# Second norm's output stored without a gap column; gated tiles stored in 64-byte steps

## The chip, the cores and the metric

One core of one Trainium2 chip runs the kernel. The metric is the time of one execution on the device in microseconds (us), taken as the median of several runs.

## The reference

One layer of a hybrid backbone for 640 tokens: 128 context tokens and 512 latent tokens, 1024 channels. A modulated norm, two token mixers (retention and attention), gates, an output projection with a residual; then a second modulated norm and a gated feed-forward part with a convolution of width 3 along the tokens, separately for context and latents; a last norm. What the change touches, cut to its core:

```python
def token_mixer(h, ...):
    ...
    y = sigmoid(ga) * (ya @ w_att_o) + sigmoid(gr) * (yr @ w_ret_o)
    return y @ w_out, ...

def conv_ffn(h, w_up, conv_w, conv_b, w_down):       # D_FF = 2816
    u = h @ w_up                                     # 1024 -> 2 x 2816
    up = jnp.pad(u, ((0, 0), (1, 1), (0, 0)))        # a zero token at both ends
    uc = conv_w[0] * up[:, :L] + conv_w[1] * up[:, 1:L + 1] + conv_w[2] * up[:, 2:L + 2] + conv_b
    a, g = jnp.split(uc, 2, axis=-1)
    return (jax.nn.silu(g) * a) @ w_down

def layer(x, ...):        # once for the context, once for the latents
    x = x + g1 * token_mixer(h, ...)
    h = rmsnorm(x, norm2_g) * (1.0 + sc2) + sh2
    x = x + g2 * conv_ffn(h, ...)
```

## The kernel before, in words

The 640 tokens are five tiles of 128: tile 0 the context, tiles 1 to 4 the latents. Both groups go through the same products at once. Each fp32 operand is split into a high part (rounded to TensorE's fp32r, a cast on ScalarE, "hi") and a low part (the rest, a subtraction on VectorE or an accumulating DMA, "lo"), and a product is three matmuls: hi x hi, hi x lo and lo x hi (`mm3`, L156 to L158).

`h2` is a pair (hi, lo) of arrays with channels on the partitions and tokens in the free dimension. It is used twice. First `merge` (L1101 to L1105) writes y into it, one block of 128 channels at a time, as the ret products of two blocks are done; the output projection then reads it as the stationary operand (`yk`), in `a_group` (first half of the output columns) and `out_half` (second half). After that, `h2_norm` and `h2_trans` write the second norm's output into it, tile by tile. It is 644 columns wide: the context at 0 to 127, a zero gap column at 128, the latents at 129 to 640, and three zero columns behind. The gap stands for the zero token between context and latents, so that one convolution over all columns serves both groups. VectorE writes these zeros once.

The feed-forward part makes 22 blocks of 128 channels of a and 22 of g. Blocks 0 and 1 of both are computed by `up_cols` in column pieces of 256 and 388 columns, as the tiles become ready; blocks 2 and 3 of a by a plain product in halves of 322 columns (`HW`); all others two at a time by `unit_group` (19 groups), seven products (m = 1, 5, 6, 2, 3, 7, 4) of four channel blocks over 322 columns in place of eight, with sums of the halves of h2 and of the weights made beforehand (`sums`, on VectorE and ScalarE; `PLAN` for the weights). Products 1, 6, 7 and 4 of a unit add up in one PSUM bank (named mm7.mm.n), which ScalarE reads in between: L1564 after m = 1, L1568 after m = 6, L1572 after m = 7 (a copy into a small constant array, const.u1), L1577 after m = 4. VectorE adds or subtracts the other terms (L1570 for m = 2, L1573 for m = 7, L1583 for m = 3). The result u is a row of 645 columns with a zero column at either end, read by `conv` (L1346 on ScalarE, L1347 and L1348 on VectorE) in 641 columns and three shifts. `gate` makes tanh (L1358), two products (L1359, L1360) and the hi and lo parts of the gated tile (L1361 on ScalarE, L1362 on VectorE) into gt0 and gt1, each of which holds a pair of blocks in 2 x 644 columns. The down projection reads tiles of 128 tokens from these as its stationary operand, four blocks at a time (`down_groups`), ten banks of 12 matmuls for each set of four blocks; `last_group` does the last four blocks. `down_sum` adds to the residual x1 on VectorE (L1435 to L1452).

TensorE's order is written out by hand: `groups` lists loads, weight preparations and product items, `seq` strings the items with m = 4 held back by two items, and `pump` lets preparations run ahead while eight weight slots (`wh`) are free. Raw weights have two slots (`raw`, loaded by SP's queue, L133), and are cast at L144 (hi) and L149 (lo), or L146 and an accumulating DMA of GpSimd (L147) for the lo part; in a unit at L1540 and L1545. In the feed-forward part a scheduler sets the order of ScalarE's and VectorE's instructions from its own costs; each engine works through its list in that order.

## Time and profile before

| what | value |
|---|---|
| median of 3 runs | 1170.83 us (1170.36 to 1171.75) |
| the profiled execution's span | 1169.8 us; about 1.0 us less than the median, which lies around the span |
| granted TensorE clock | 9 tenths or more of full speed in all 40 slices |
| PE, DVE, ACT, POOL busy | 98%, 66%, 51%, 15% of the span |
| output projection | about 657 to 720 us |
| second norm, first pairs of up-projection | about 690 to 770 |
| first down banks | 770 to 784 |
| units and down banks | 784 to 1130 |
| last down banks, residual, last norm | 1130 to the end |

PE is TensorE's matmuls, PEld its weight loads, DVE VectorE, ACT ScalarE, POOL GpSimd, SP SyncE; a q behind the name is the engine's queue. A row of the timeline has the start in us from the span's beginning, the duration, engine, line, operation, output <- inputs, the shape, and in brackets the idle time just before it and what ended that. Matmuls overlap, so their cost is read from start to start and not from the duration. The chain of waits is followed back from the last instruction: each piece is a start, a length and the work on which the rest waited.

### The profile page before, as it was taken

What the parts mean: (1) busy time and instruction counts of PE and PEld (TensorE: products, weight loads), DVE (VectorE), ACT (ScalarE), POOL (GpSimd) and SP (SyncE); (2) the same over time, 40 slices, a digit from 0 to 9 for tenths busy, and PEclk for the clock granted to TensorE, in tenths of its full rate; (3) what the DMA queues carried; (4) which work ended last, traced back from release to release, by engine and by line L of the source; (5) the groups of instructions that cost most, each with busy time, mean ns of one, the idle gap of its engine ahead of it and who ended that gap; (6) DMA issues with size and microseconds to landing.
All of it is one profiled execution on the core that took longest, in us unless ns stands there. A gap on an engine that the chain in (4) does not pass through costs nothing.

```text
span 1169.8 us, 18399 instructions
## 1 busy us (share of the span) xinstructions
PE 1143.2 (98%) x7269; PEld 1030.1 (88%) x7269; DVE 772.8 (66%) x1433; ACT 591.5 (51%) x1087; POOL 180.8 (15%) x194
## 2 busy tenths in 40 slices
...
PEclk9999999999999999999999999999999999999999
...
GB/s 306 244 136 72 38 36 37 37 35 217 261 175 171 176 76 76 37 37 36 71 38 148 267 110 200 110 83 124 153 132 134 143 136 168 127 117 153 136 110 125
DMA packets 135848, 145.85 MB, mean 125 GB/s; under 512 B 26561, under 2 KB 101393, under 8 KB 135761
## 3 DMA queue, kind: packets, MB, share of 16 engines
...
q8 instruction: 57, 0.93, 0.3%
...
## 4 chain that ended last, share of the span: by engine, by line
PE 80%; DVE 8%; ACT 5%; issue 3%; DMA 2%; POOL 1%; ACTq 0%; DVEq 0%; POOLq 0%
DMA f1.s.11_5326<-spill.u2.2_2889 1%; DMA f1.s.13_5328<-spill.u2.2_2889 1%; DVE x1.u1.1_6460 L1440 1%; DMA weights.raw.414_10840<-in_w_down 0%; POOL f0.s.5_3528 L955 0%; DMA const.u2.2_72<-in_b_mod 0%; DVE x1.u1.1_6460 L1489 0%; DVE x1.u1.1_6460 L1452 0%; ACT acts.u1.1_91 L1104 0%; DVE gt.gt0.5_7309 L1388 0%; DVE weights.raw.395_10492 L1537 0%; DVE x1.u1.1_6460 L1447 0%; DVE acts.u2.2_92 L414 0%; PE mm1.mm.11_295 L158 0%; PE mm7.mm.42_9455 L1559 0%
## 5 line engine op out<-in xcount | busy, mean ns | idle before, releaser
L796 POOL DMA_DIRECT2D spill.u2.2_2889<-f1.s.1_1161 x1 | 0.6, 588 | 130.2 <-DVE mod.u4.4_2848 L587 130.2
L1573 DVE TENSOR_TENSOR t7.u4.4_6978<-t7.u4.4_6978,const.u1.1_70 128x322 f32<-128x322 f32 x10 | 5.0, 496 | 11.8 <-ACT const.u1.1_70 L1572 11.8
L1085 POOL DMA_DIRECT2D weights.wh.164_5980<-weights.raw.156_5913 x1 | 1.3, 1347 | 69.6 <-DVE f1.s.9_5324 L1125 69.6
L892 DVE SCALAR_TENSOR_TENSOR ret2.u1.1_4325<-ret2.u1.1_4325,const.u13.13_88 64x128 f32<-64x128 f32 x24 | 6.8, 339 | 6.6 <-ACT ret2.u1.1_4325 L885 6.5
L894 DVE SCALAR_TENSOR_TENSOR ret2.u1.1_4325<-ret2.u1.1_4325,const.u13.13_88 64x128 f32<-64x128 f32 x24 | 6.6, 386 | 4.8 <-ACT ret2.u1.1_4325 L887 4.8
L842 DVE TENSOR_TENSOR ret.u5.5_3531<-ret.u5.5_3531,ret.u1.1_3524 128x512 f32<-128x512 f32 x5 | 3.5, 692 | 9.4 <-POOL ret.r2k.8_3709 L840 3.3
L842 DVE TENSOR_TENSOR ret.u4.4_3530<-ret.u4.4_3530,ret.u1.1_3524 128x512 f32<-128x512 f32 x5 | 3.5, 692 | 9.0 <-POOL ret.r2k.11_3889 L840 4.7
L566 POOL TENSOR_TENSOR p1.u1.1_605<-p1.u3.3_609,p1q.u1.1_599 128x512 f32<-128x512 f32 x1 | 1.3, 1310 | 43.9 <-DMA p1.u4.4_611<-in_cache_k 43.9
L149 DVE TENSOR_TENSOR weights.wh.108_4359<-weights.raw.106_4356,weights.wh.107_4358 128x1024 fp32r<-128x1024 f32 x1 | 1.2, 1224 | 10.3 <-ACT weights.wh.107_4358 L144 10.3
L144 ACT CAST weights.wh.112_4514<-weights.raw.111_4512 128x1024 fp32r<-128x1024 f32 x1 | 1.1, 1050 | 13.2 <-PE mm3.mm.36_4223 L157 13.2
L411 ACT CAST acts.u1.1_91<-f0.s.2_105 128x640 fp32r<-128x640 f32 x4 | 2.9, 728 | 9.5 <-DVE f0.s.2_105 L409 9.5
L259 DVE COPY mod2.wr.9_4315<-aux3.aux.15_4282 128x128 f32<-128x128 f32 x1 | 0.3, 291 | 10.9 <-PE aux3.aux.15_4282 L256 10.9
L428 PE MATMUL aux1.aux.1_135<-const.u1.1_70,const.u2.2_72 80*128 80x80 f32 x1 | 0.4, 365 | 7.0 <-DMA const.u2.2_72<-in_b_mod 7.0
L955 POOL TENSOR_TENSOR f0.s.5_3528<-f0.s.5_3528,ret2.ny20.13_4911 128x512 f32<-128x512 f32 x5 | 6.0, 1236 | 8.0 <-DVE ret2.ny20.13_4911 L219 8.0
L535 ACT ACTIVATE f0.s.3_711<-f0.s.3_711,p1q.ny20.11_879 128x128 f32<-128x128 f32 x20 | 6.0, 388 | 2.5 <-DVE p1q.ny20.11_879 L217 2.5
L144 ACT CAST weights.wh.67_3362<-weights.raw.66_3360 128x1024 fp32r<-128x1024 f32 x1 | 1.0, 1045 | 11.5 <-PE mm3.mm.8_3141 L195 11.5
L144 ACT CAST weights.wh.77_3617<-weights.raw.76_3615 128x1024 fp32r<-128x1024 f32 x1 | 1.0, 1045 | 11.5 <-PE mm3.mm.16_3454 L195 11.5
L144 ACT CAST weights.wh.72_3542<-weights.raw.71_3540 128x1024 fp32r<-128x1024 f32 x1 | 1.0, 1045 | 11.4 <-PE mm3.mm.12_3298 L195 11.4
L1451 DVE TENSOR_TENSOR x1.u1.1_6460<-x1.u1.1_6460,gate.u1.1_6447 128x512 f32<-128x512 f32 x10 | 6.8, 686 | 0.0
L144 ACT CAST weights.wh.92_3979<-weights.raw.91_3977 128x1024 fp32r<-128x1024 f32 x1 | 1.0, 1047 | 11.2 <-PE mm3.mm.26_3760 L157 11.2
L861 POOL MEMSET ret2.u2.2_4326<- 128x512 f32 x1 | 0.5, 525 | 38.9 <-PE aux3.aux.15_4282 L256 38.9
L1484 POOL TENSOR_TENSOR x1.u1.1_6460<-x1.u1.1_6460,weights.raw.422_11041 128x512 f32<-128x512 f32 x3 | 4.9, 1649 | 10.2 <-ACT x1.tm.112_11054 L1457 7.4
...
## 6 DMA issues: line engine op xcount, KB each, us to landing
...
p0.u6.6_126<-in_w_mod SPq DMA_DIRECT2D x2, 1024.0 KB, 15.2
p0.u7.7_129<-in_w_mod SPq DMA_DIRECT2D x2, 1024.0 KB, 12.1
...
```

The lines of the kernel that those rows point to most:

```text
L144: nc.scalar.copy(hi, rv)
L411: nc.scalar.copy(hT[0][:, k, :], xk)
L535: nc.scalar.activation(x[:, j], x[:, j], AF.Copy, scale=rstd[:, j:j + 1])
L566: nc.gpsimd.tensor_mul(ct, r2[:, :, 0, :], gqk[:, i:i + 1, :].to_broadcast([P, 4, P]))
L842: V.tensor_mul(z, z, r1[:, t, 0:1, :].to_broadcast([P, 8, 64]))
L892: V.scalar_tensor_tensor(Ss[0:64, hh, st + 1, j], Ss[0:64, hh, st, j], cdsel[0:64, h:h + 1], Ss[0:64, hh, st + 1, j], op0=ALU.mult, op1=AL ...
L894: V.scalar_tensor_tensor(Ss[64:128, hh, 2 - st, j], Ss[64:128, hh, 3 - st, j], cdsel[64:128, h:h + 1], Ss[64:128, hh, 2 - st, j], op0=ALU. ...
L955: nc.gpsimd.tensor_mul(ov, ov, rso[:, 4 * t:4 * t + 4].unsqueeze(2).to_broadcast([P, 4, P]))
L1440: V.tensor_add(x1[:, t, gs], x1[:, t, gs], down_mul(ps, t, c0))
L1451: V.tensor_mul(x1[:, t, gs], x1[:, t, gs], gb[:, t == 0, gs])
L1484: eng.tensor_mul(x, x, fg[:, c0:c0 + 512])
L1573: V.tensor_sub(u[1][:, hi_u], u[1][:, hi_u], u3[i])
```

## The change

`HW` becomes 320, and h2 has 640 columns without a gap.

- `merge` casts and subtracts a block of 640 columns in one instruction each, in place of 128 and 512.
- The zeroing of the gap columns (a memset and four copies on VectorE) goes.
- The output projection's tiles start at t x 128 in place of one column on, and so do the second norm's.
- `up_cols` computes 256 and 384 columns; the plain product and the units 2 x 320. The gap exists only in u: `u_parts` cuts a piece of columns that spans column 128 in two, so the lower half (0 to 319) is written as 128 + 192 columns by two instructions: on ScalarE for m = 1 and m = 6, on VectorE for m = 2 and m = 3.
- Zero columns of u are written once at the start by GpSimd (12 memsets in place of 4); VectorE's memsets behind m = 3, 7 and 4 go.
- The gated tiles lie in rows of 656 columns (`GW`), shifted by 15 columns: the latents' tiles start at 16 + 128 t columns, and the second block of a pair 656 columns on, which in bytes are multiples of 64; the context's tile starts at column 15. Before, they were at 0 and 129 + 128 (t - 1), the second block 644 on.

```diff
@@ shapes
-HW = 322
+HW = 320
+GW = 656
...
@@ def a_group
-                ts = slice(t * P + gap * (t > 0), (t + 1) * P + gap * (t > 0))
+                ts = slice(t * P, (t + 1) * P)
...
@@ def merge(f)
             c = 2 * p + f
-            for s_, d_ in ((slice(0, P), slice(0, P)), (slice(P, TOK), slice(P + 1, TOK + 1))):
-                nc.scalar.copy(h2[0][:, c, d_], u[f][:, s_])
-                V.tensor_sub(h2[1][:, c, d_], u[f][:, s_], h2[0][:, c, d_].bitcast(F32))
+            nc.scalar.copy(h2[0][:, c, :], u[f])
+            V.tensor_sub(h2[1][:, c, :], u[f], h2[0][:, c, :].bitcast(F32))
...
@@ def gt_pair()
-        return [gtp([P, 2, 2 * HW], F32R, tag=f"gt{i}", bufs=2) for i in range(2)]
+        return [gtp([P, 2, GW], F32R, tag=f"gt{i}", bufs=2) for i in range(2)]
...
@@ def h2_trans(t)
-        c0 = t * P + int(t > 0)
+        c0 = t * P
...
@@ ahead of out_half
-    zero = x_tmp()[:, :KD * 4].rearrange("p (k c) -> p k c", k=KD)
-    V.memset(zero, 0)
-    for h in h2:
-        V.tensor_copy(h[:, :, P:P + 1], zero[:, :, :1])
-        V.tensor_copy(h[:, :, TOK + 1:], zero[:, :, 1:])
@@ def out_half(t, h)
-            ts = slice(t * P + (t > 0), (t + 1) * P + (t > 0))
+            ts = slice(t * P, (t + 1) * P)
...
-            nc.gpsimd.memset(u[:, 0:1], 0)
+            for c in (0, P + 1, TOK + 2):
+                nc.gpsimd.memset(u[:, c:c + 1], 0)
+
+    def u_parts(u, lo, hi):
+        cuts = [lo] + [P] * (lo < P < hi) + [hi]
+        return [(u[:, x + 1 + (x >= P):y + 1 + (x >= P)], slice(x - lo, y - lo)) for x, y in zip(cuts, cuts[1:])]
...
@@ def up_cols
-        nc.scalar.copy(ub[f % 2][i][:, lo + 1:hi + 1], ps)
+        for d, sl in u_parts(ub[f % 2][i], lo, hi):
+            nc.scalar.copy(d, ps[:, sl])
...
@@ def gate(f)
-        r = [x[:, f % 2, :641] for x in gts[f // 2]]
+        r = [x[:, f % 2, 15:656] for x in gts[f // 2]]
...
@@ def down_mm
-        c0 = 0 if t == 0 else 129 + (t - 1) * P
+        c0 = 15 if t == 0 else 16 + t * P
...
@@ unit_group: def prod(m)
-        lo_u, hi_u = slice(1, 1 + HW), slice(1 + HW, 1 + 2 * HW)
+        los = [u_parts(x, 0, HW) for x in u]
+        his = [u_parts(x, HW, TOK)[0][0] for x in u]
...
                 if m == 1:
-                    nc.scalar.copy(u[0][:, lo_u], ps)
+                    for d, sl in los[0]:
+                        nc.scalar.copy(d, ps[:, sl])
...
                 elif m == 6:
-                    nc.scalar.activation(u[1][:, lo_u], ps, AF.Copy, scale=-1.0)
+                    for d, sl in los[1]:
+                        nc.scalar.activation(d, ps[:, sl], AF.Copy, scale=-1.0)
                 elif m == 2:
-                    V.tensor_add(u[0][:, lo_u], u[0][:, lo_u], ps)
+                    for d, sl in los[0]:
+                        V.tensor_add(d, d, ps[:, sl])
                 elif m == 7:
                     nc.scalar.copy(u3[i], ps)
-                    V.tensor_sub(u[1][:, hi_u], u[1][:, hi_u], u3[i])
-                    V.memset(u[1][:, 642:643], 0)
+                    V.tensor_sub(his[1], his[1], u3[i])
...
                 elif m == 4:
-                    nc.scalar.copy(u[0][:, hi_u], ps)
-                    V.memset(u[0][:, 642:643], 0)
+                    nc.scalar.copy(his[0], ps)
...
                 else:
-                    V.tensor_sub(u[1][:, lo_u], u[1][:, lo_u], ps)
-                    V.memset(u[1][:, 129:130], 0)
+                    for d, sl in los[1]:
+                        V.tensor_sub(d, d, ps[:, sl])
```

Behind the change lines move by one to five: L1346 is L1348, L1361 and L1362 are L1363 and L1364, L1572 and L1573 are L1578 and L1579, L144 is L145.

TensorE's and SP's orders are the same but for the sizes. ScalarE's and VectorE's lists change in length (ScalarE 939 to 971 rows, VectorE 1339 to 1307) and at a few places in order. Three of them follow.

ScalarE, where the first gate copies (L276) follow the sums of the halves, about 753 us (sums.u5 is the high part of a sum of halves of h2, x1.row the convolution's result). Before:

```order
L144 CAST weights.wh.219_7364<-weights.raw.215_7355 128x1024
L1339 COPY t7.u4.4_6978<-mm3.mm.92_7234 128x388
L1401 CAST sums.u5.5_6970<-gt.gt0.5_7309 128x1288
L1346 ACTIVATE x1.row.60_7273<-t7.u4.4_6978,t7.u5.5_6983 128x641
L276 COPY gate.u1.1_6447<-mm7.mm.1_7285 128x512
L276 COPY gate.u1.1_6447<-mm7.mm.2_7291 128x512
```

After:

```order
L145 CAST weights.wh.219_7354<-weights.raw.215_7345 128x1024
L1341 COPY t7.u4.4_6956<-mm3.mm.92_7224 128x384
L147 ACTIVATE weights.wh.220_7355<-weights.raw.215_7345 128x1024
L1348 ACTIVATE x1.row.59_7263<-t7.u4.4_6956,t7.u5.5_6969 128x641
L277 COPY gate.u1.1_6431<-mm7.mm.1_7275 128x512
L277 COPY gate.u1.1_6431<-mm7.mm.2_7281 128x512
L1403 CAST sums.u5.5_6948<-gt.gt0.5_7299 128x1280
```

The cast of the sum has moved behind two gate copies, and a weight's low part stands in its place.

ScalarE in the units, about 819 us, between the copy of an m = 7 product and the next m = 1 copies (u is t7.u1 to u4). Before:

```order
L1572 COPY const.u1.1_70<-mm7.mm.15_7859 128x322
L1346 ACTIVATE x1.row.67_7987<-t7.u4.4_6978,t7.u5.5_6983 128x641
L1564 COPY t7.u1.1_6975<-mm7.mm.18_7991 128x322
L144 CAST weights.wh.252_8033<-weights.raw.247_7895 128x1024
L146 ACTIVATE weights.wh.253_8034<-weights.raw.247_7895 128x1024
```

After:

```order
L1578 COPY const.u1.1_70<-mm7.mm.15_7854 128x320
L145 CAST weights.wh.252_8029<-weights.raw.247_7891 128x1024
L1348 ACTIVATE x1.row.66_7983<-t7.u4.4_6956,t7.u5.5_6969 128x641
L1568 COPY t7.u1.1_6953<-mm7.mm.18_7987 128x128
L1568 COPY t7.u1.1_6953<-mm7.mm.18_7987 128x192
L147 ACTIVATE weights.wh.253_8030<-weights.raw.247_7891 128x1024
```

The weight's cast has moved ahead of the convolution, and the m = 1 copy is two.

ScalarE behind the last unit's m = 6 product, where the last raw weights (raw.414) are cast. Before:

```order
L1568 ACTIVATE t7.u4.4_6978<-mm7.mm.63_10822 128x322
L1572 COPY const.u1.1_70<-mm7.mm.63_10822 128x322
L144 CAST weights.wh.416_10891<-weights.raw.414_10840 128x1024
L1346 ACTIVATE x1.row.109_10938<-t7.u4.4_6978,t7.u5.5_6983 128x641
L144 CAST weights.wh.418_11031<-weights.raw.407_10724 128x1024
L146 ACTIVATE weights.wh.419_11032<-weights.raw.407_10724 128x1024
L144 CAST weights.wh.420_11036<-weights.raw.414_10840 128x1024
L1577 COPY t7.u2.2_6976<-mm7.mm.63_10822 128x322
L1358 ACTIVATE t7.tg.26_10983<-x1.row.109_10938 128x641
L1346 ACTIVATE x1.row.110_10970<-t7.u2.2_6976,t7.u5.5_6983 128x641
L146 ACTIVATE weights.wh.421_11037<-weights.raw.414_10840 128x1024
```

After:

```order
L1573 ACTIVATE t7.u4.4_6956<-mm7.mm.63_10833 128x192
L145 CAST weights.wh.416_10903<-weights.raw.414_10852 128x1024
L1578 COPY const.u1.1_70<-mm7.mm.63_10833 128x320
L145 CAST weights.wh.418_11042<-weights.raw.407_10734 128x1024
L147 ACTIVATE weights.wh.419_11043<-weights.raw.407_10734 128x1024
L1348 ACTIVATE x1.row.108_10950<-t7.u4.4_6956,t7.u5.5_6969 128x641
L145 CAST weights.wh.420_11047<-weights.raw.414_10852 128x1024
L1582 COPY t7.u2.2_6954<-mm7.mm.63_10833 128x320
L147 ACTIVATE weights.wh.421_11048<-weights.raw.414_10852 128x1024
L1348 ACTIVATE x1.row.109_10981<-t7.u2.2_6954,t7.u5.5_6969 128x641
L1360 ACTIVATE t7.tg.26_10994<-x1.row.108_10950 128x641
```

The m = 7 copy has moved behind the cast of wh.416, and the convolution and tanh behind further casts. On VectorE the subtraction that reads that copy has moved behind the low part of the same weights. Before:

```order
L1573 TENSOR_TENSOR t7.u4.4_6978<-t7.u4.4_6978,const.u1.1_70 128x322
L1574 MEMSET t7.u4.4_6978 128x1
L149 TENSOR_TENSOR weights.wh.417_10892<-weights.raw.414_10840,weights.wh.416_10891 128x1024
L1347 SCALAR_TENSOR_TENSOR x1.row.109_10938<-t7.u4.4_6978,t7.u5.5_6983,x1.row.109_10938 128x641
L1348 SCALAR_TENSOR_TENSOR x1.row.109_10938<-t7.u4.4_6978,t7.u5.5_6983,x1.row.109_10938 128x641
```

After:

```order
L150 TENSOR_TENSOR weights.wh.417_10904<-weights.raw.414_10852,weights.wh.416_10903 128x1024
L1579 TENSOR_TENSOR t7.u4.4_6956<-t7.u4.4_6956,const.u1.1_70 128x320
L1349 SCALAR_TENSOR_TENSOR x1.row.108_10950<-t7.u4.4_6956,t7.u5.5_6969,x1.row.108_10950 128x641
L1350 SCALAR_TENSOR_TENSOR x1.row.108_10950<-t7.u4.4_6956,t7.u5.5_6969,x1.row.108_10950 128x641
L1349 SCALAR_TENSOR_TENSOR x1.row.109_10981<-t7.u2.2_6954,t7.u5.5_6969,x1.row.109_10981 128x641
```

Here wh.417 now comes ahead of the subtraction and the convolution behind both; x1.row.108 and 109 after are 109 and 110 before.

10 lines of the change are left out of this document (5 added, 5 removed).

## The prediction, made before the changed kernel was run

> **What bounds the kernel now.** The page comes first: the share of TensorE (PE), its clock, and who makes up the chain that ended last.
>
> ```profile
> PE 1143.2 (98%) x7269; PEld 1030.1 (88%) x7269; DVE 772.8 (66%) x1433; ACT 591.5 (51%) x1087; POOL 180.8 (15%) x194
> PEclk9999999999999999999999999999999999999999
> PE 80%; DVE 8%; ACT 5%; issue 3%; DMA 2%; POOL 1%; ACTq 0%; DVEq 0%; POOLq 0%
> ```
>
> Next the windows by stage (from:to, length, then busy time of PE, PEld, DVE, ACT, POOL, clock, DMA share, GB/s).
>
> ```profile
> 784.00:884.00 100.00, 99.87 (x606) 93.93 (x606) 77.49 (x135) 65.58 (x113) 18.11 (x16) 1.00 0.60 132
> 984.00:1084.00 100.00, 100.00 (x575) 91.72 (x574) 78.78 (x136) 57.23 (x97) 16.36 (x14) 1.00 0.64 143
> 1134.00:1170.00 36.00, 26.18 (x125) 21.24 (x124) 28.72 (x53) 16.21 (x35) 8.64 (x8) 0.92 0.40 117
> ```
>
> From 784 to 1084 PE is full at a granted clock of 1.00, while ACT and DVE have 20 to 40 us in 100 to spare: there a matmul saved is time saved. The end is different, as the chain of waits shows:
>
> ```profile
> 1091.21 0.16 PE mm7.mm.57_10456 L1562
> 1091.40 0.44 ACT const.u1.1_70 L1572
> ...
> 1125.55 0.61 DVE x1.row.108_10874 L1347
> 1126.15 5.13 DMA weights.raw.414_10840<-in_w_down
> 1131.28 0.02 issue
> 1131.31 1.05 ACT weights.wh.416_10891 L144
> ...
> 1143.61 0.84 DVE gt.gt1.28_10982 L1362
> ```
>
> The chain leaves PE at 1091.40 and runs by ACT, DVE and one weight load to the last gated tile, 1144.45. So PE time saved before 1091 counts: DVE and ACT then start their last stretch sooner, and the load, which waits for DVE at 1126.15, goes out sooner with them. PE time saved after 1091 doesn't count, and ACT and DVE work between the load's landing (1131.31) and 1144.45 counts in full. The waits of PE's weight loads, 600 to the end (line, releaser: total, times, longest us), name the larger stalls that are left, three before 1091 and one (acc.51) in the end itself:
>
> ```profile
> PEld acc7.acc.11_8140 L158 <- DVE gt.gt1.12_8069 L1362: 0.6, 1, 0.6
> PEld acc7.acc.51_10942 L158 <- DVE gt.gt1.28_10982 L1362: 0.6, 1, 0.6
> PEld mm7.mm.5_7371 L1336 <- ACT gate.u1.1_6447 L276: 0.4, 1, 0.4
> PEld aux3.aux.90_6532 L274 <- ACT gate.u1.1_6447 L276: 0.4, 1, 0.4
> ```
>
> **Columns.** What the change removes first is two columns of every matmul over h2. PE's timeline (start, duration) has the 322-column products of the feed-forward part and the 320-column products of an earlier stage, both in gapless runs:
>
> ```profile
> 561.75 0.31 PE L194 MATMUL mm3.mm.49_5476<-acts.u1.1_91,weights.wh.134_5338 128*128 128x320 f32 x1
> 608.83 0.31 PE L1114 MATMUL mm3.mm.63_5899<-yr.u1.1_5318,weights.wh.152_5832 128*128 128x320 f32 x1
> ...
> 783.69 0.31 PE L1559 MATMUL mm7.mm.9_7597<-acts.u1.1_91,weights.wh.222_7483 128*128 128x322 f32 x1
> 831.51 0.40 PE L156 MATMUL acc7.acc.11_8140<-weights.wh.252_8033,gt.gt0.9_7787 128*128 128x512 f32 x1
> ```
>
> 321 matmuls start in the first 47.08 us, 146.67 ns each; 324 in the second 47.82, 147.59 each. The difference is 0.92 ns a matmul, 11.0 ns a product of 12, and the ratio is 322/320 to four digits. Of 19 x 7 = 133 products 126 lie before 1091.40: **1.39 us**. The plain up group's 96 matmuls add **0.09**. (The Trainium skill, "TensorE: Matmul & The Clock Gate", Back-to-back issue gap, has a warm gap of N/2.4 + 2.5 ns, so 0.83 ns for two columns; the sum would be 1.26 in place of 1.39. The rows are nearer to pure proportion.)
>
> **Alignment.** Runs of 512-column matmuls, from a start to the first row behind the run:
>
> ```profile
> 525.95 0.39 PE L156 MATMUL mm3.mm.44_5150<-weights.wh.122_5155,acts.u1.1_91 128*128 128x512 f32 x1
> 548.14 0.30 PE L194 MATMUL mm3.mm.47_5346<-acts.u1.1_91,weights.wh.132_5334 128*128 128x320 f32 x1
> ...
> 676.81 0.40 PE L156 MATMUL mm3.mm.75_6473<-weights.wh.190_6448,acts.u1.1_91 128*128 128x512 f32 x1
> 690.75 0.40 PE L156 MATMUL mm3.mm.80_6679<-weights.wh.194_6647,acts.u1.1_91 128*128 128x512 f32 x1
> ...
> 769.83 0.39 PE L156 MATMUL acc7.acc.1_7502<-weights.wh.216_7357,gt.gt0.7_7325 128*128 128x512 f32 x1
> ...
> 839.40 0.39 PE L156 MATMUL acc7.acc.13_8190<-weights.wh.252_8033,gt.gt0.9_7787 128*128 128x512 f32 x1
> 847.78 0.31 PE L1559 MATMUL mm7.mm.21_8240<-acts.u1.1_91,weights.wh.259_8090 128*128 128x322 f32 x1
> ```
>
> With tiles at multiples of 128 columns (525.95) 96 matmuls take 22.19 us, 2774 ns per 12. The output projection, whose tiles stand one column on (676.81), has 60 in 13.94: 2788. The down banks (839.40) have 36 in 8.38: 2793. But the first down banks, 769.83 to 783.69, read tiles just as shifted and take 60 in 13.86: 2772. So alignment is one candidate for these 14 to 19 ns and not a proven one. If it is the cause, the 240 matmuls of the output projection give back 0.28 and the 35 four-f down banks before 1091 give 0.67; if not, nothing. I take **0.2** of 0 to 0.28, since the whole run there is slow, and **0.35** of 0 to 0.67, half, because of the contrary run. The Trainium skill, "SBUF — State Buffer", Operand start alignment, says of element alignment that "This is about legality, not speed"; it knows no such price, and by it both terms would be nothing.
>
> **Merges, splits and gates** on ACT:
>
> ```profile
> 665.54 0.82 ACT L1104 CAST acts.u1.1_91<-f1.s.13_5328 128x128 fp32r<-128x128 f32 x2 [4.71 <-DMA f1.s.13_5328<-spill.u2.2_2889]
> 667.71 1.04 ACT L144 CAST weights.wh.190_6448<-weights.raw.188_6438 128x1024 fp32r<-128x1024 f32 x1
> ...
> 750.48 1.05 ACT L146 ACTIVATE weights.wh.217_7358<-weights.raw.210_7343 128x1024 fp32r<-128x1024 f32 x1
> 752.79 1.27 ACT L1401 CAST sums.u5.5_6970<-gt.gt0.5_7309 128x1288 fp32r<-128x1288 f32 x1
> ...
> 819.30 0.43 ACT L1572 COPY const.u1.1_70<-mm7.mm.15_7859 128x322 f32<-128x322 f32 x1 [0.67 <-PE mm7.mm.15_7859 L1562]
> 820.30 0.93 ACT L1346 ACTIVATE x1.row.67_7987<-t7.u4.4_6978,t7.u5.5_6983 128x641 f32<-128x641 f32 x1 [0.56 <-DVE t7.u4.4_6978 L1573]
> L411 ACT CAST acts.u1.1_91<-f0.s.2_105 128x640 fp32r<-128x640 f32 x4 | 2.9, 728 | 9.5 <-DVE f0.s.2_105 L409 9.5
> L861 POOL MEMSET ret2.u2.2_4326<- 128x512 f32 x1 | 0.5, 525 | 38.9 <-PE aux3.aux.15_4282 L256 38.9
> ```
>
> The change makes one cast of each pair of merge casts. Three split merges take 665.54 to 667.71, 0.72 each. One 640-wide cast is 0.73 long (L411) and steps some 0.1 less than it lasts (665.54's pair lasts 0.82 and steps 0.72), so 0.63: one split costs 0.09 of ACT, at most 0.19 if nothing overlaps. The last three merges stand ahead of the weight casts and gate copies for which PE waits 0.4 at L274; fused, those come 0.27 sooner. Upstream, the subtraction can now start only behind a whole cast, so I take **0.15** (0 to 0.4, the whole wait). The zeroing of the gap columns that goes from DVE at the same place is five small instructions on an engine that PE does not wait for there, and counts nothing; so do the eight more memsets on GpSimd, which the windows show busy 16 to 24 us in 100: they stand ahead of the first u, and if something waited for them they would cost at most 8 x 0.53, what L861's memset of 512 columns takes.
>
> At 755 PE waits 0.4 for a gate copy behind conv and the 1288-wide cast of 1.27. In the order after, a 1024-wide cast (1.05) stands there in place of it: **0.22** less (0 to 0.4). This contains the 0.18 that the 384-column blocks save, which PE would otherwise spend waiting.
>
> At 819.73 ACT stands idle 0.56 for DVE's L1573. In the order after, the cast of wh.252 fills this hole, and the gated tile for which PE waits 0.6 at 834 comes sooner by about that: **0.4** (0 to 0.6). What is late next is the next gated tile of the same group, and its bank runs one bank, 2.8 us, later. Elsewhere the 38 split reads of PSUM cost ACT 38 x 0.09 = 3.4 us, DVE about what the dropped memsets return; the spare time in the windows covers it. If that cover were gone, it is rival three.
>
> **The end.** The order moves more than the columns do. Before:
>
> ```profile
> 1130.20 0.43 ACT L1572 COPY const.u1.1_70<-mm7.mm.63_10822 128x322 f32<-128x322 f32 x1 [4.84 <-PE mm7.mm.63_10822 L1562]
> 1132.27 0.92 ACT L1346 ACTIVATE x1.row.109_10938<-t7.u4.4_6978,t7.u5.5_6983 128x641 f32<-128x641 f32 x1
> ...
> 1130.66 0.50 DVE L1573 TENSOR_TENSOR t7.u4.4_6978<-t7.u4.4_6978,const.u1.1_70 128x322 f32<-128x322 f32 x1 [1.56 <-ACT const.u1.1_70 L1572]
> 1132.39 1.23 DVE L149 TENSOR_TENSOR weights.wh.417_10892<-weights.raw.414_10840,weights.wh.416_10891 128x1024 fp32r<-128x1024 f32 x1 [1.11 <-ACT weights.wh.416_10891 L144]
> ```
>
> The m=7 copy and DVE's subtraction were done by 1131.16, inside the load's wait, and conv ran straight behind the cast. After, the copy stands behind that cast, so it ends at landing + 1.4, and DVE takes wh.417 first (to +2.2) and the subtraction to +2.7; ACT does two more casts (to +3.2) and only then conv (+4.1), a cast (+5.0), the m=4 copy (+5.3), a cast (+6.3), the other conv (+7.1) and its tanh (+7.8). From there DVE sets the pace with six instructions of 0.83 to 0.87 before the last high half's cast (0.74) and the last low half (0.84): about 14.45 behind the landing, where it was 13.14 (1144.45 - 1131.31). I take **-1.3** (0 if another engine's delay hides it; -1.6 if one step more falls between). PE's m=4 product adds onto the bank that the copy reads and so queues behind it; the last low half is still later than that, so PE's wait there costs nothing of its own.
>
> **Sum.** 1.39 + 0.09 + 0.2 + 0.35 + 0.15 + 0.22 + 0.4 - 1.3 = 1.50 less. The profiled span is 1169.8, about 1.0 under the median of 1170.83, so 1168.3 in the span and **1169.3** as a median. What can be told from no change is 0.2%, 2.3 us.
>
> **Rivals.** *The end is not longer* (0.30): the copy's place costs nothing, because DVE, which is saturated ahead of the landing, is late in any case. Then 1168.0; with all of the alignment (another 0.4) 1167.6. Against it: DVE waited 1.56 for that copy, and 1.11 for the cast. *Columns alone* (0.14): no alignment gain, 0.55 less: 1169.8. For it speaks the run at 769.83. (This is what the Trainium skill's sentence above comes to.) *ACT becomes the pace* (0.08): the splits between 784 and 1091 delay the u tiles, conv and gates, so that PE waits for gated tiles at every down group as it did once at 834. It decides once the extra 0.18 us per group exceeds the spare time ahead of each down group. Then the 3.4 us show, the column gain is lost in waiting, and the end costs 1.3, against some 1.2 of the other gains: +3.5, 1174.3. Against it: ACT is busy 66 in 100 there.
>
> **Chances.** Forecast 0.48, rivals 0.30, 0.14, 0.08. Faster by over 0.2% (under 1168.5) is the first rival and the forecast's lower edge: 0.37. Slower: the third, 0.08. The rest, 0.55, is within. The range is 1167.3 to 1170.7: from the first rival with all of the alignment, and 0.3 more from the stalls' upper bounds, to the forecast without alignment, without the gate at 834 and the merges, and with the end at -1.6.
>
> **What would show it.** Products start to start at 1760 ns per 12 (the column term). Output projection and down banks at 2774 (alignment) or still at 2788 to 2793. PE's waits for L276's copies and for the gated tile at 834 shorter. At the end: the m=7 copy behind the cast of wh.416, the last low half 14.4 behind the landing, and PE's last wait for gt1 over 1.5 us. A wait for ACT inside the products, or a wait at every down group, would make the prediction wrong.

## The result, and the profile after

The changed kernel takes 1166.65 us (median of 6, 1166.27 to 1168.41), the kernel before 1170.96 in the runs beside it (1170.36 to 1171.75): a ratio of 0.9966, 95% interval 0.9954 to 0.9977. That is faster by 4.3 us and below the range of the prediction, which forecast 1169.3. The profiled execution took 1167.02, its span 1165.2; the span before was 1169.8.

The page of the changed kernel, with the rows that answer to those of before (busy time and share by engine, the clock, and the chain that ended last):

```profile
PE 1136.6 (98%) x7269; PEld 1026.4 (88%) x7269; DVE 771.0 (66%) x1401; ACT 592.4 (51%) x1123; POOL 181.9 (16%) x202
PEclk9999999999999999999999999999999999999999
PE 81%; DVE 7%; ACT 5%; issue 3%; DMA 3%; POOL 1%; ACTq 0%; DVEq 0%; POOLq 0%; SPq 0%
```

The windows by stage (from:to, length, then busy time of PE, PEld, DVE, ACT, POOL, clock, DMA share, GB/s):

```profile
784.00:884.00 100.00, 99.86 (x611) 94.12 (x611) 78.52 (x131) 66.14 (x126) 18.93 (x16) 1.00 0.65 137
984.00:1084.00 100.00, 100.00 (x586) 92.47 (x585) 78.11 (x128) 57.79 (x106) 16.40 (x14) 1.00 0.62 140
```

PE has 6.6 us less to do with the same 7269 matmuls, and is as full as before: 611 matmuls now fit where 606 did. ScalarE has 36 instructions more and is busy 0.9 us longer, far from full. So far this is the forecast's picture. What the page doesn't tell is where PE's time went, and for that the same matmul's start is read in both timelines. Every row below is a stretch between two matmuls that exist in both kernels, named by the place before:

| from | to | what lies in it | before | after | gain |
|---|---|---|---|---|---|
| 0 | 548.14 | all stages up to there | 548.14 | 544.71 | 3.43 |
| 548.14 | 676.81 | 320-column products of the earlier stage | 128.67 | 128.63 | 0.04 |
| 676.81 | 724.14 | output projection | 47.33 | 46.35 | 0.98 |
| 724.14 | 727.92 | last transposes of h2 | 3.78 | 4.20 | -0.42 |
| 727.92 | 769.83 | up blocks and plain up group | 41.90 | 41.35 | 0.55 |
| 769.83 | 783.69 | first down banks | 13.86 | 13.89 | -0.03 |
| 783.69 | 1091.20 | units and down banks | 307.51 | 305.56 | 1.95 |
| 1091.20 | end | the end | 78.64 | 80.55 | -1.91 |

The gains sum to 4.59, the difference of the spans (1169.84 and 1165.25 unrounded). **Three quarters of it, 3.43, comes from stages in which the diff changes no instruction.** These are PE's rows there after the change (start, duration):

```profile
522.95 0.39 PE L157 MATMUL mm3.mm.44_5150<-weights.wh.122_5155,acts.u1.1_91 128*128 128x512 f32 x1
525.67 0.39 PE L157 MATMUL mm3.mm.45_5151<-weights.wh.122_5155,acts.u1.1_91 128*128 128x512 f32 x1
...
544.71 0.30 PE L195 MATMUL mm3.mm.47_5346<-acts.u1.1_91,weights.wh.132_5334 128*128 128x320 f32 x1
...
673.34 0.39 PE L157 MATMUL mm3.mm.75_6457<-weights.wh.190_6432,acts.u1.1_91 128*128 128x512 f32 x1
686.94 0.39 PE L157 MATMUL mm3.mm.80_6657<-weights.wh.194_6631,acts.u1.1_91 128*128 128x512 f32 x1
...
779.14 0.30 PE L1562 MATMUL mm7.mm.9_7589<-acts.u1.1_91,weights.wh.222_7475 128*128 128x320 f32 x1
826.65 0.39 PE L157 MATMUL acc7.acc.11_8137<-weights.wh.252_8029,gt.gt0.9_7782 128*128 128x512 f32 x1
834.40 0.40 PE L157 MATMUL acc7.acc.13_8186<-weights.wh.252_8029,gt.gt0.9_7782 128*128 128x512 f32 x1
842.74 0.31 PE L1562 MATMUL mm7.mm.21_8236<-acts.u1.1_91,weights.wh.259_8088 128*128 128x320 f32 x1
```

The first three rows are the surprise: 96 matmuls from 522.95 to 544.71 take 21.76 us, 2720 ns per 12, where the same 96 took 22.19 (2774) before. The granted clock is 1.00 in both. All 1080 matmuls of this kind ahead of 548.14 take 259.91 us before and 256.53 after, so they hold 3.38 of the 3.43. The output projection's 60 take 13.60 (2720, before 2788), the down banks' 36 take 8.34 (2780, before 2793). The products step as forecast: 324 in 47.51 us, 146.6 ns each.

The end, in the chain of waits of the changed kernel:

```profile
1113.88 6.45 DMA weights.wh.410_10793<-weights.raw.397_10521
1120.39 5.06 DMA weights.raw.414_10852<-in_w_down
1125.47 1.05 ACT weights.wh.416_10903 L145
1126.53 0.32 ACT const.u1.1_70 L1578
1126.84 0.95 ACT weights.wh.418_11042 L145
1127.80 0.95 ACT weights.wh.419_11043 L147
1128.75 0.81 ACT x1.row.108_10950 L1348
...
1139.01 0.84 DVE gt.gt1.28_10993 L1364
```

The cast of wh.416 starts at 1125.47 and the last gated tile is done at 1139.84 (1139.01 and 0.83 of the instruction itself): 14.37 behind it, where it was 13.14 before. And the raw weights land only 5.84 sooner than before (1131.31), although PE's last unit ran 6.50 sooner (1091.20 to 1084.70): their load waits for an accumulating transfer of 6.45 us, issued at 1113.88; the same one was issued at 1120.42 before and took 5.67, and there, too, the load went out as it landed (1126.15).

The waits of PE's weight loads from 600 to the end (total, times, longest):

```profile
PEld acc7.acc.51_10954 L157 <- ACT gt.gt0.27_10992 L1363: 1.3, 1, 1.3
PEld acc7.acc.51_10954 L159 <- DVE gt.gt1.28_10993 L1364: 0.8, 2, 0.6
PEld mm3.mm.74_6356 L1117 <- DMA weights.wh.180_6226<-weights.raw.168_6021: 0.7, 1, 0.7
...
PEld acc7.acc.11_8137 L159 <- DVE gt.gt1.12_8066 L1364: 0.6, 1, 0.6
PEld aux3.aux.98_7029 L1260 <- ACT x1.row.46_6909 L1270: 0.5, 1, 0.5
...
PEld mm7.mm.5_7361 L1337 <- ACT gate.u1.1_6431 L277: 0.3, 1, 0.3
```

The wait of 0.6 for gt1.12 is as long as before, so that term of the forecast failed. The wait of 0.5 at aux3.aux.98 is new: it is the -0.42 in the table. The wait for a DMA at mm3.mm.74 belongs to that execution: it is 0.3, 1.3 or absent in other profiles of the same stage below.

### The profile page after: what moved, and what is told of

Its sections match the earlier page's. It is cut to its first block, busy times and chain, and to the rows that moved or that the text cites. A ratio compares the mean times of both kernels' runs of the same rounds, so it can differ in the third digit from the quotient of the medians.

```text
span 1165.2 us, 18448 instructions
## 1 busy us (share of the span) xinstructions
PE 1136.6 (98%) x7269; PEld 1026.4 (88%) x7269; DVE 771.0 (66%) x1401; ACT 592.4 (51%) x1123; POOL 181.9 (16%) x202
## 4 chain that ended last, share of the span: by engine, by line
PE 81%; DVE 7%; ACT 5%; issue 3%; DMA 3%; POOL 1%; ACTq 0%; DVEq 0%; POOLq 0%; SPq 0%
DMA weights.wh.180_6226<-weights.raw.168_6021 1%; DMA weights.wh.410_10793<-weights.raw.397_10521 1%; DVE x1.u1.1_6444 L1442 1%; DMA weights.raw.247_7891<-in_w_down 0%; DMA weights.raw.414_10852<-in_w_down 0%; POOL f0.s.5_3528 L956 0%; DMA const.u2.2_72<-in_b_mod 0%; DVE x1.u1.1_6444 L1491 0%; DVE x1.u1.1_6444 L1240 0%; DVE acts.u2.2_92 L1272 0%; DVE acts.u2.2_92 L415 0%; PE mm1.mm.11_295 L159 0%; PE mm7.mm.12_7704 L1565 0%; PE mm7.mm.57_10464 L1564 0%; PE mm7.mm.33_8972 L1564 0%
## 5 line engine op out<-in xcount | busy, mean ns | idle before, releaser
L1579 DVE TENSOR_TENSOR t7.u4.4_6956<-t7.u4.4_6956,const.u1.1_70 128x320 f32<-128x320 f32 x10 | 4.9, 492 | 9.8 <-ACT const.u1.1_70 L1578 9.8
L145 ACT CAST weights.wh.112_4514<-weights.raw.111_4512 128x1024 fp32r<-128x1024 f32 x1 | 1.1, 1050 | 13.0 <-PE mm3.mm.36_4223 L158 13.0
L145 ACT CAST weights.wh.67_3362<-weights.raw.66_3360 128x1024 fp32r<-128x1024 f32 x1 | 1.0, 1045 | 11.5 <-PE mm3.mm.8_3141 L196 11.5
L145 ACT CAST weights.wh.77_3617<-weights.raw.76_3615 128x1024 fp32r<-128x1024 f32 x1 | 1.0, 1045 | 11.5 <-PE mm3.mm.16_3454 L196 11.5
L145 ACT CAST weights.wh.72_3542<-weights.raw.71_3540 128x1024 fp32r<-128x1024 f32 x1 | 1.0, 1045 | 11.4 <-PE mm3.mm.12_3298 L196 11.4
L145 ACT CAST weights.wh.92_3979<-weights.raw.91_3977 128x1024 fp32r<-128x1024 f32 x1 | 1.1, 1055 | 11.0 <-PE mm3.mm.26_3760 L158 11.0
```

Of the source, the lines that this page charges most:

```text
L145: nc.scalar.copy(hi, rv)
L1579: V.tensor_sub(his[1], his[1], u3[i])
```

## The experiments

Two questions were open: what made matmuls of 512 columns 4.5 ns shorter in a stage that the diff doesn't touch, and what the other terms were worth.

For the first question, the two kernels were compared in the one thing that differs there: where the arrays lie. The arrays hold 8 x 2 x HW columns of four bytes each: 20608 bytes before, 20480 after. In the allocation of the compiled programs the weight tiles lie at 320 modulo 512 bytes in both kernels, and so does the high part of h; the low part of h, allocated behind the high part, lies at 448 before and at 320 after. In the stages up to 548 both kernels read h in rows of 640 columns (2560 bytes, 5 x 512), with tiles of 128 columns (512 bytes). So there every stationary tile lies like its array, and before, the low part alone lay unlike the weights that stream past it. The theory: a matmul is longer when its stationary tile and the operand that streams past it do not lie alike modulo 512 bytes. The rivals: the 512-byte grid itself (an absolute address), a step of 64 bytes, a stationary tile that lies unlike the one loaded before it (high and low part take turns), or something else that the change brought. Beside the runs below the kernel before took 1170.96 to 1171.44 us as a median, so the times of different experiments compare to about half a us.

**The kernel before with its arrays padded to 41 x 512 bytes.** Nothing else is changed; no matmul has fewer columns.

```diff
-    hflat = [hp([P, KD * 2 * HW], F32R) for _ in range(2)]
+    hflat = [hp([P, 5248], F32R)[:, :KD * 2 * HW] for _ in range(2)]
```

> Edit: the kernel before, with 5248 columns (41 x 512 bytes) allocated for each of the two h arrays, so that the low array starts at the same address modulo 512 bytes as the high array and the weights. Nothing else moves in order or size. Theory R (a 512-column matmul costs more when its stationary tile lies elsewhere modulo 512 bytes than the weights it streams): the first norm's products before 548 us go from 2774 to 2720 ns per 12, the stage ends about 3.4 us sooner, the output projection (tiles still one column on, rows still 644 apart) stays near 2788, the time is about 1167.5. Rival (the gain before 548 us came from something else in the change): 2774 stays, 1170.9.

Measured: 1168.23 us, ratio to before 0.9971 (0.996 to 0.9982). PE's timeline:

```profile
522.63 0.40 PE L156 MATMUL mm3.mm.44_5150<-weights.wh.122_5155,acts.u1.1_91 128*128 128x512 f32 x1
544.40 0.30 PE L194 MATMUL mm3.mm.47_5346<-acts.u1.1_91,weights.wh.132_5334 128*128 128x320 f32 x1
```

These 96 take 21.77, as after the change. The padding alone, in the kernel before, gives the whole of the first stage's gain (548.14 to 544.40, 3.74), and all 1080 matmuls of the kind take 256.60. The output projection, whose tiles stand one column on, stays slow there: 13.92 for its 60.

**The changed kernel with its arrays 64 bytes longer.** This puts the low part at 384 modulo 512, 64 bytes from where the weights lie.

```diff
-    hflat = [hp([P, KD * 2 * HW], F32R) for _ in range(2)]
+    hflat = [hp([P, KD * 2 * HW + 16], F32R)[:, :KD * 2 * HW] for _ in range(2)]
```

> Edit: the changed kernel, with 16 columns (64 bytes) more allocated for each h array, so that the low array starts 64 bytes off the high array and the weights, modulo 512. Theory R: the excess returns in the first products and in the output projection, 2720 goes to about 2770 ns per 12, and some 4 us are lost: 1170.5 to 1171. Rival (multiples of 64 bytes are enough, as the gated tiles' layout has it): 2720 stays, 1166.7.

Measured: 1169.63, ratio 0.9985 (0.9976 to 0.9994). Some 2.5 to 3 of the 4.3 us gained are gone, less than the 4 that were expected, with every other part of the change in place:

```profile
525.69 0.39 PE L157 MATMUL mm3.mm.44_5150<-weights.wh.122_5155,acts.u1.1_91 128*128 128x512 f32 x1
547.87 0.30 PE L195 MATMUL mm3.mm.47_5346<-acts.u1.1_91,weights.wh.132_5334 128*128 128x320 f32 x1
```

22.18 for the 96 (2773 per 12), and the output projection's 60 are at 13.87. So steps of 64 bytes are not enough.

**Everything 64 bytes on.** A constant ahead of the arrays is made longer, so that weights and both parts of h move together.

```diff
-    sso = cp([P, 2, NT, 4])
+    sso = cp([P, 8 * NT + 16])[:, :8 * NT].rearrange("p (a t c) -> p a t c", a=2, c=4)
```

> Edit: the changed kernel, with 64 bytes more allocated ahead of weights and h, so that all of them move by 64 bytes together, the gated tiles not. Theory R in its relative form (stationary against streamed operand): 2720 stays, 1166.7. Absolute form (only 320 modulo 512 bytes, as it happens to be, is good): about 2770 ns per 12 in the first products and the output projection, and 4 us or more lost, 1170.5 or above.

Measured: 1166.63, ratio 0.9958 (0.9943 to 0.9973), as the changed kernel:

```profile
522.36 0.39 PE L157 MATMUL mm3.mm.44_5150<-weights.wh.122_5155,acts.u1.1_91 128*128 128x512 f32 x1
```

The run ends at 544.12, 21.76 later. It is the place of one operand against the other that counts, not the place itself.

**Everything 32 bytes on.** The same, by half: weights and h lie at 352 modulo 512, no longer a multiple of 64.

```diff
-    sso = cp([P, 2, NT, 4])
+    sso = cp([P, 8 * NT + 8])[:, :8 * NT].rearrange("p (a t c) -> p a t c", a=2, c=4)
```

> Edit: the changed kernel, with 32 bytes more allocated ahead of weights and h, so that all of them start at 352 modulo 512 bytes, alike but at no multiple of 64; the gated tiles stay. If lying alike is enough: 2720 ns per 12 in the first products and the output projection, 1166.7, as with 64 bytes more. If a multiple of 64 is needed as well: up to 2770, and up to 4.5 us lost, 1171.

Measured: 1167.14, ratio 0.9963 (0.995 to 0.9976):

```profile
523.68 0.40 PE L157 MATMUL mm3.mm.44_5150<-weights.wh.122_5155,acts.u1.1_91 128*128 128x512 f32 x1
545.45 0.30 PE L195 MATMUL mm3.mm.47_5346<-acts.u1.1_91,weights.wh.132_5334 128*128 128x320 f32 x1
```

21.77. A multiple of 64 isn't needed either; lying alike is.

**Both parts of h moved, the weights left in place.** So far the low part had always moved against the weights and against the high part at once. Here both parts go 64 bytes on inside arrays that are 512 bytes longer, so tiles that follow each other still lie alike, but none lies like the weights.

```diff
-    hflat = [hp([P, KD * 2 * HW], F32R) for _ in range(2)]
+    hflat = [hp([P, KD * 2 * HW + 128], F32R)[:, 16:16 + KD * 2 * HW] for _ in range(2)]
```

> The changed kernel with both parts of h 64 bytes on (384 modulo 512), the weights left where they are (320). So the stationary tiles that follow each other still lie alike, but none lies like the weights that stream past it. Theory (the tile against the streamed operand decides): the 96 matmuls from mm3.mm.44 to mm3.mm.47 take 22.2 to 22.5 us (2774 to 2810 per 12, since now all three of a kind are unlike and not one), the output projection's 60 take 13.9 to 14.0, and the time is 1169.5 to 1172. Rival (a tile against the tile before it decides): 21.76 and 13.60 as in the changed kernel, time 1166.6. The products of 320 columns, with the weights as tiles, stay at 146.6 ns by the rival, and step longer by the theory if it held for every matmul.

Measured: 1172.16, ratio 1.0009 (0.9999 to 1.0019): the whole gain of the change is gone, and 5.5 us against the changed kernel.

```profile
527.52 0.39 PE L157 MATMUL mm3.mm.44_5150<-weights.wh.122_5155,acts.u1.1_91 128*128 128x512 f32 x1
549.92 0.31 PE L195 MATMUL mm3.mm.47_5346<-acts.u1.1_91,weights.wh.132_5334 128*128 128x320 f32 x1
...
784.59 0.31 PE L1562 MATMUL mm7.mm.9_7589<-acts.u1.1_91,weights.wh.222_7475 128*128 128x320 f32 x1
832.04 0.39 PE L157 MATMUL acc7.acc.11_8137<-weights.wh.252_8029,gt.gt0.9_7782 128*128 128x512 f32 x1
```

The 96 take 22.40 us, 2800 per 12 and 233.3 ns each, since now every tile is unlike, and all 1080 of the kind 261.73; the output projection's 60 take 14.00. So it is the tile against the streamed operand, and not against the tile before it. The 324 products of 320 columns take 47.45, as in the changed kernel (47.51), although h, which they stream, has moved against the weights, which are their tiles. What is shown for 512 columns doesn't hold for these.

**The same by 256 bytes** (64 in place of 16 columns):

```diff
-    hflat = [hp([P, KD * 2 * HW], F32R) for _ in range(2)]
+    hflat = [hp([P, KD * 2 * HW + 128], F32R)[:, 64:64 + KD * 2 * HW] for _ in range(2)]
```

> The same with both parts of h 256 bytes on (64 modulo 512, weights at 320). Theory with 512 bytes as the period: as with 64 bytes, 22.2 to 22.5 us for the 96, time 1169.5 to 1172. If the period is 256 bytes: 21.76, time 1166.6, although 64 bytes cost. Rival (a tile against the tile before it): 21.76 and 1166.6 in both kernels.

Measured: 1166.63, ratio 0.9956 (0.9942 to 0.9971), as the changed kernel:

```profile
522.25 0.39 PE L157 MATMUL mm3.mm.44_5150<-weights.wh.122_5155,acts.u1.1_91 128*128 128x512 f32 x1
544.01 0.30 PE L195 MATMUL mm3.mm.47_5346<-acts.u1.1_91,weights.wh.132_5334 128*128 128x320 f32 x1
```

21.76. The period is therefore 256 bytes, not 512, and not 128 either, since before the change the low part lay just 128 off.

**The gated tiles made to lie like the weights.** The change puts its latents' tiles at steps of 64 bytes, at 0, 64, 128 and 192 modulo 256 by buffer and row (the weights are at 64); only one in four of these lies like the weights. With rows of 768 columns (3072 bytes) and the latents' tiles from column 64 on, all of them lie at 320 modulo 512, as the weights do, but the context's, which stands one column ahead.

```diff
-GW = 656
+GW = 768
-        r = [x[:, f % 2, 15:656] for x in gts[f // 2]]
+        r = [x[:, f % 2, 63:704] for x in gts[f // 2]]
-        c0 = 15 if t == 0 else 16 + t * P
+        c0 = 63 if t == 0 else 64 + t * P
```

> Edit: the changed kernel, with the gated tiles in rows of 768 columns and shifted by 63 in place of 15, so that the latents' tiles start at the same address modulo 512 bytes as the weights; the context's tile stays off by 4 bytes. Theory R: the down banks of the latents go from about 2793 to 2720 ns per 12, those of the context stay; 32 banks before the end save about 2.2 us, 1164.5. Rival (the down banks are slow for another reason, such as the products between them): 2793 stays, 1166.7.

Measured: 1164.75, ratio 0.994 (0.9924 to 0.9957), 1.9 under the changed kernel. The same 36 matmuls of the down banks:

```profile
833.61 0.39 PE L157 MATMUL acc7.acc.13_8186<-weights.wh.252_8029,gt.gt0.9_7782 128*128 128x512 f32 x1
841.80 0.30 PE L1562 MATMUL mm7.mm.21_8236<-acts.u1.1_91,weights.wh.259_8088 128*128 128x320 f32 x1
```

8.19 where they were 8.34. Sorted by tile, the matmuls of the tiles that lie like the weights step by 227.5 ns on the average, those of the context tile, four bytes off, by 233: both kinds in one kernel, at one clock. Between 784 and 1091 the down banks go from 97.92 to 96.57 us.

**The gated tiles back where they were before the change** (rows of 644, tiles at columns 0 and 129), run once:

```diff
-GW = 656
+GW = 644
-        r = [x[:, f % 2, 15:656] for x in gts[f // 2]]
+        r = [x[:, f % 2, :641] for x in gts[f // 2]]
-        c0 = 15 if t == 0 else 16 + t * P
+        c0 = 0 if t == 0 else 129 + (t - 1) * P
```

> Edit: the changed kernel, with the gated tiles back in the layout of before (rows of 644 columns, context at 0, latents at 129). Theory R (steps of 64 bytes are worth nothing unless the tiles lie like the weights modulo 512 bytes): the down banks stay at 2790 to 2800 ns per 12, 1166.7. Rival (the 64-byte steps brought part of the gain): the down banks get slower than with the change.

Measured: 1168.80, a single run. The down banks' matmuls without the stalls step by 232.1 ns, in the changed kernel by 231.9: on some 420 matmuls the 64-byte steps are worth 0.1 us. The padded kernel before, whose gated tiles stand where they stood against the weights (modulo 256 bytes), has 97.95 us for the same 420, where the change has 97.92 and the kernel before 98.36: the 0.44 comes without the 64-byte steps as well. That execution is longer because PE waited for gated tiles and a copy, not because its matmuls were longer:

```profile
PEld acc7.acc.41_10345 L157 <- ACT gt.gt0.23_10273 L1363: 0.9, 1, 0.9
...
PEld acc7.acc.41_10345 L159 <- DVE gt.gt1.24_10274 L1364: 0.6, 1, 0.6
PEld mm7.mm.51_10062 L1562 <- ACT t7.u2.2_6954 L1568: 0.4, 1, 0.4
```

Whether these waits come from the tiles' place or from that one execution isn't settled by one run.

**The merges split again.**

```diff
-            nc.scalar.copy(h2[0][:, c, :], u[f])
-            V.tensor_sub(h2[1][:, c, :], u[f], h2[0][:, c, :].bitcast(F32))
+            for s_ in (slice(0, P), slice(P, TOK)):
+                nc.scalar.copy(h2[0][:, c, s_], u[f][:, s_])
+                V.tensor_sub(h2[1][:, c, s_], u[f][:, s_], h2[0][:, c, s_].bitcast(F32))
```

> Edit: the changed kernel, with each merge cast and subtraction again in two pieces of 128 and 512 columns, without a gap. Theory: the gate copies about 666 us come 0.2 to 0.3 later and TensorE waits there 0.4 again, as before the change; the total moves by less than 0.4 since what is waited for next hides it. Rival: the merges brought more than that, and over 1 us is lost by 690.

Measured: 1168.02, a single run. The wait of 0.4 at L274, which the forecast meant the fused merges to shorten, isn't there after the change, but it does not come back with the split merges either. The waits of PE's weight loads from 600 to 770 in this kernel:

```profile
PEld mm3.mm.74_6364 L1118 <- DMA weights.wh.180_6228<-weights.raw.168_6021: 1.3, 1, 1.3
PEld aux3.aux.98_7045 L1261 <- ACT x1.row.46_6925 L1271: 0.5, 1, 0.5
PEld mm3.mm.66_6024 L1115 <- ACT f1.s.12_5327 L1124: 0.5, 1, 0.5
```

In two of the kernels with fused merges (both parts of h 256 bytes on, and the last of the attention runs below) the wait is there again, 0.5 each. So it comes and goes with something other than the merges, which isn't known, and the merges are worth next to nothing here. Of the 1.0 by which this profiled execution is longer than the changed kernel's, 0.6 is the DMA wait at mm3.mm.74 (1.3 in place of 0.7), which the merges don't feed, and 0.5 lies in the end, behind the first matmul of the row "the end".

**The end in the order that it was written.** Here the preparation of wh.416 is held back until the last m = 7 product is issued, and from there on ScalarE's order is the written one.

```diff
+    late, lpos = groups[-1][1][0][0], pos[id(groups[-3][2][5])] + 1
...
-            elif preps and preps[0][0] < loaded and sum(z for z, last in live if last >= n) + preps[0][2] <= 8:
+            elif preps and preps[0][0] < loaded and (preps[0][1] is not late or n >= lpos) and sum(z for z, last in live if last >= n) + preps[0][2] <= 8:
...
+    with tc.manual_schedule(engines={ET.PE, ET.Activation}):
+        walk(cut, len(seq))
+        for fn in later:
+            fn()
```

> Edit: the changed kernel, with ScalarE's order of before at the end: the preparation of wh.416 is held until the last m = 7 product is issued and ScalarE follows the written order from there, so the m = 7 copy stands ahead of that cast and the convolution straight behind it. Theory (the order costs the end): the last low half comes about 13.1 us behind the landing of the last weights in place of 14.4, the wait of TensorE for the m = 7 copy (0.7) goes, and the time falls by 1.2 to 1.9 us to 1164.8 to 1165.4. Rival (the end is slower for another reason, such as the load that comes later after TensorE's gain): 1166.7.

Measured: 1168.24, ratio 0.9972 (0.9961 to 0.9983): it was expected to be faster than the changed kernel, and is 1.6 slower by the medians. The copy was done ahead of the landing and the convolution ran straight behind the cast, but the gates came in a worse order (the second tanh behind the first gated tile's cast), and the last low half was done 14.84 behind the landing. PE's wait now stood in one piece:

```profile
PEld acc7.acc.51_10962 L157 <- ACT gt.gt0.27_11000 L1363: 2.2, 1, 2.2
```

The windows around it show a second price, the clock (0.57, the third figure from the end):

```profile
1136.00:1139.00 3.00, 1.45 (x6) 0.63 (x4) 2.39 (x3) 1.15 (x3) 0.00 (x0) 1.00 0.49 179
1139.00:1143.00 4.00, 3.64 (x9) 2.54 (x10) 2.21 (x3) 0.80 (x2) 0.00 (x0) 0.57 0.02 4
1143.00:1147.00 4.00, 4.00 (x19) 3.25 (x18) 3.53 (x5) 1.44 (x5) 1.28 (x1) 1.00 0.00 0
```

Nine matmuls run in the four us behind the wait, and 19 in the next four. From the last low half to the end of the span it takes 26.66 us, in the changed kernel 25.41.

**The order of before on ScalarE and VectorE at the end,** instruction by instruction, and nothing else of the change undone (the convolution and the gate are issued in steps so that casts can stand between them):

```diff
+    with tc.manual_schedule(engines={ET.PE, ET.Activation, ET.DVE}):
+        while later:
+            later.pop(0)()
+        seq[cut]()
...
+        conv(NF - 1, 1)
+        ends[0][3]()
+        e1 = ends[1][4]()
+        next(e1)
+        seq[m4]()
+        ga, gb_, cb = gate_steps(NF - 1), gate_steps(NF - 2), conv_steps(NF - 2, 1)
...
```

> Edit: the changed kernel, with the order of before on ScalarE and on VectorE from the last m = 7 product to the last gated tile, instruction by instruction (the run before restored only the copy, the cast and the first convolution). Theory (the reordered gates cost the end 1.24): the last low half ends 13.1 us behind the landing of the last weights, as before the change, in place of 14.4; TensorE's clock does not fall, since its wait is shorter than in that run; 1165.4. Rival (what the order gives is taken back by TensorE, as in that run): 1166.5 or more.

Measured: 1165.73, ratio 0.9951 (0.9934 to 0.9967), 0.9 under the changed kernel by the medians; the intervals of the two ratios overlap, so the evidence is in the trace. VectorE at the end:

```profile
1136.06 0.83 DVE L1374 TENSOR_TENSOR x1.row.107_10885<-x1.row.107_10885,x1.row.109_10997 128x641 f32<-128x641 f32 x1
1137.68 0.83 DVE L1378 TENSOR_TENSOR gt.gt1.28_10993<-x1.row.107_10885,gt.gt0.27_10992 128x641 fp32r<-128x641 f32 x1 [0.79 <-ACT gt.gt0.27_10992 L1376]
```

The last low half is done at 1138.51, 13.13 behind the cast of wh.416 (1125.38): before it was 13.14. The order alone makes the 1.24.

**A better order there, together with the aligned gated tiles.** The casts that need no new data (wh.418 and 419) go ahead of the last m = 7 product's copy, and that copy and its convolution ahead of the cast that waits for the load.

```diff
+    with tc.manual_schedule(engines={ET.PE, ET.Activation, ET.DVE}):
+        ends[0][3]()
+        seq[cut]()
+        while later:
+            later.pop(0)()
+        pump(cut + 1)
+        for n in range(cut + 1, m4):
+            seq[n]()
+        ga = gate_a(NF - 1)
+        seq[m4]()
+        while later:
+            later.pop(0)()
+        ends[1][3]()
+        gate_b(NF - 1, ga)
+        gate(NF - 2)
```

> Edit: the kernel with gated tiles in rows of 768 columns (1164.75), with a written order for ScalarE and VectorE at the end: the two casts of wh.418 and 419 before the last m = 7 product (ScalarE stands idle 6.5 us there), the m = 7 copy and the convolution ahead of the cast that waits for the last load, and the other convolution and the tanh as soon as their inputs are there. If the gates' chain behind the last load sets the end, the last low half comes about 11 us behind the landing and 2.5 to 3 us go: about 1162. If another wait takes over at once, less than 1 us goes.

Measured: 1162.71, ratio 0.9928 (0.9913 to 0.9943): 3.9 under the changed kernel and 8.4 under the one before. The last low half is done 9.76 behind the landing, 4.6 sooner than in the changed kernel, and PE waits for no gated tile there, so only 2.0 of that shows in the time (1164.75 to 1162.71). All waits of its weight loads from 1100 on:

```profile
PEld mm7.mm.64_10854 L1572 <- DMA weights.wh.410_10793<-weights.raw.397_10521: 0.6, 1, 0.6
PEld mm7.mm.64_10854 L1569 <- PE mm7.mm.63_10833 L1572: 0.3, 1, 0.3
```

**The same rule tried on the attention.** Its matmuls, too, step 5 to 8 ns over the best. First one array was made longer so that the transposed probabilities and the values lie alike (both at 480), then the values' second array 160 bytes longer on top of it, so that both lie at 320.

```diff
-    gqk = tq([P, 2, P])
+    gqk = tq([P, 2 * P + 112])[:, :2 * P].rearrange("p (a d) -> p a d", a=2)
```

> Edit: the fastest kernel so far (1162.71), with 448 bytes more ahead of the attention's tiles, so that the transposed probabilities start like the values they are multiplied with, modulo 512 bytes (480 against 480; before 416 against 480). Theory R, in a stage that the change doesn't touch: the 512-column matmuls there lose their 5 to 8 ns of excess, 0.8 us over all of them, 1161.9, or less where TensorE waits for the softmax. Rival (the rule holds only for weights and h): no change.

```diff
-    vv = [kvp([P, 6, 256], F32R) for _ in range(2)]
+    vv = [kvp([P, 6, 256], F32R), kvp([P, 6 * 256 + 40], F32R)[:, :6 * 256].rearrange("p (b d) -> p b d", b=6)]
```

> Edit: the fastest kernel so far (1161.92), with 160 bytes more allocated behind the attention's values, so that values and transposed probabilities both start at 320 modulo 512 bytes, a multiple of 64, in place of 480, which is none. In the run before they already lay alike, and yet kept 5 to 8 ns of excess. If lying alike and a multiple of 64 bytes are both needed, the excess goes to about 1 ns and 0.7 us go: 1161.2. If the attention's excess has another cause (the products around it, the work on the other engines), 5 to 8 ns stay, 1161.9.

Measured: 1161.92, ratio 0.9921 (0.9906 to 0.9936), and 1161.95, ratio 0.9919 (0.9902 to 0.9936). Neither can be told from the kernel without the padding, and the attention's matmuls keep their excess: 5 to 8 ns in the first, 4 to 7.6 in the second. So nearly all of that excess has another cause, and it stays open.

## Why the prediction missed

The time was forecast 2.6 us too long. By the forecast's own steps:

- **Columns: right in mechanism, with a miscount.** The forecast put 126 products ahead of 1091.40; the trace has 118 there, which is 1.30 at its 11.0 ns each in place of 1.39. Measured: 1.50 (209.15 to 207.65 us for their 1416 matmuls, 147.7 to 146.6 ns each, stalls included).
- **Alignment: the step that failed.** The prediction took the run at 525.95 as the place where operands are aligned ("With tiles at multiples of 128 columns (525.95) 96 matmuls take 22.19 us, 2774 ns per 12") and measured the others against it. That run was itself slow. Its tiles stand at multiples of 512 bytes within their array, but the low array's own base lay 128 bytes off the weights; with both alike the run is at 2720, with both parts unlike at 2800. Two errors follow from this one. The output projection was allowed 0.28 at most, and its runs of 60 gained 0.34 each; the stretch from 676.81 to 724.14 gained 0.98. And a stage that the diff doesn't name got no term at all, though the change shortens the arrays from 40 x 512 + 128 bytes to 40 x 512, and this shifts the low part: 3.43 us. The 1080 matmuls of that kind gained 3.1 ns each on the mean and not the 4.5 of the run at 525.95: without the 75 to 78 stalled steps of over 250 ns, which stayed, they went from 231.4 to 227.8.
- **The contrary run** at 769.83 (2772, "tiles just as shifted") looked like evidence against any price. It was no contradiction: it and the reference were unaligned alike. With the gated tiles at 768 columns it takes 13.65 us for its 60, 2730 per 12.
- **Down banks: right by luck.** 0.35 was forecast for them, 0.44 came (98.36 to 97.92, stalls included), but within the changed kernel the 64-byte steps bring about 0.1, and the padded kernel before gets nearly the same (97.95) without them; what brings it is open. Placed like the weights the tiles bring 1.35 more.
- **Merges** 0.15: the wait that they were to shorten did go, but splitting them again didn't bring it back, and two kernels with fused merges have it (0.5), so the forecast's reason fails and the cause isn't shown.
- **Up group and gate copies** 0.09 and 0.22: the stretch from 727.92 to 769.83 gained 0.55; of the stall itself, 0.50 became 0.36.
- **The gated tile at 834** 0.4: failed. PE's wait for it is 0.6 as before; the whole gap in PE's starts there went from 0.50 to 0.43. The cast fills the hole on ScalarE as the order showed, but PE waits for VectorE's L1364 there, and for that as long as before.
- **The end** -1.3: right in mechanism and size. 14.45 was forecast from landing to the last low half, 14.37 came, and the order of before brings 13.13 back. The forecast had a wait wrong ahead of that: it let the load wait for VectorE's L1347 at 1126.15, but that instruction ended at 1126.35, behind the load's start, and what SyncE waited for was the accumulating transfer, which landed at 1126.09. This transfer took 5.67 us before (5.63 in the padded kernel before) and 6.45 after (6.00 to 6.94 in the other variants of the changed kernel; why, no run shows), so the landing moved by 0.66 less than PE. That makes the -1.91 of the table. PE's last wait of over 1.5 us came in two, 1.3 and 0.8.
- **A new wait** at the last transposes of h2: the matmuls ahead of it are done sooner, ScalarE's L1270 isn't, and 0.42 of the projection's gain is given back there. In the kernels whose projection stays slow (13.87 to 14.00 for the 60) the stretch takes 3.75 to 3.92, as before. It is the sort of loss for which the forecast had looked only at the units.

Of the rivals, *the end is not longer* falls by the 1.24 us that its order costs, *columns alone* by the output projection's runs, and *ACT becomes the pace* by ScalarE's 66.14 us in 100 and by waits of no more than 0.2 at the down groups behind the first, up to 1091. None of them held the first stage's gain either: all four cases shared the wrong reference.

On the alignment the Trainium skill, "SBUF — State Buffer", Operand start alignment, says "This is about legality, not speed", and the prediction read it as a reason to expect no price. As a sentence on legality it stands, and it claims no more; read as the prediction read it, it fails, since 64 bytes alone move 96 matmuls from 21.76 to 22.40 us. The skill goes further in "TensorE: Matmul & The Clock Gate", Step-by-step: what each phase is for: loading the next tile's weights takes no read bandwidth from the running matmul, because the two have ports of their own. No run here shows the ports or what is short when a matmul is longer, but the step is not free of the address: where the tile lies against the streamed operand changes the step by up to 6.7 ns in 227, and the time of this kernel by 5.5 us (1172.16 against 1166.65, with both parts of h 64 bytes on).
